# Closing of a hybrid decoder layer: sample outputs stored feature by token, feature tiles transposed two down tiles behind

## The chip, the core and the metric

The kernel runs on one core of a Trainium2 chip. Five engines work side by side and meet through semaphores: PE (TensorE, products and transposes into PSUM), DVE (VectorE), ACT (ScalarE), POOL (GpSimd) and SP (SyncE, which here only issues DMA transfers). The metric is device time in microseconds, the median of several executions. A trace of one execution gives each instruction's start and duration; its first instruction to its last is the span.

## The reference

One layer of a decoder serves 512 prompt tokens and 32 sample tokens (8 sequences of 4) with shared weights. The part that matters here is the end of the layer, the second feed-forward network with its norms:

```
def rmsnorm(x, g):
    y = xf * lax.rsqrt(jnp.mean(xf * xf, axis=-1, keepdims=True) + EPS)
    return (y * g.astype(jnp.float32)).astype(x.dtype)

def swiglu(x, wg, wu, wd):
    return (jax.nn.silu(x @ wg) * (x @ wu)) @ wd

    h = h + rmsnorm(m, norm_g[3])
    h = h + 0.5 * rmsnorm(swiglu(rmsnorm(h, norm_g[4]), wg[1], wu[1], wd[1]), norm_g[5])
```

The model width is 1024 and the inner width 2816, all in 32-bit floats. The results are the tokens' new rows (512 x 1024 for the prompt, 32 x 1024 for the samples) and caches and states that are stored much earlier in the program.

## The kernel before

**Layout.** Activations lie feature by token: 1024 features are 8 tiles of 128 partitions, and tokens run along the free dimension. The 544 tokens are cut in two halves. Half a has 256 prompt tokens and is finished and stored first, still feature by token (`y_a`). Half b has 256 prompt tokens and the 32 sample tokens behind them, 288 columns, and is the last work of the program. Its prompt outputs `y_p` and its sample outputs `y_s` are stored token by feature, so its feature tiles have to be transposed on PE.

**Products.** Each product of two 32-bit matrices is made of three passes over parts: weights are split on chip into a high part `wh` (a cast on ACT, L248) and a low part `wl` (a subtraction on DVE, L249), activations in the same way (`uhb`, `ulb` and, inside the network, `hhb`, `hlb` by L168 and L169). `mm3` (L257) then issues high by high, low by high and high by low for each of the 128-deep slices: 24 products for a gate or up tile (8 slices), 15 for a tile of the last down chunk (5 slices).

**The second feed-forward network of half b** (`ffn` with `fin`): the inner width is cut in four chunks of 6, 6, 5 and 5 tiles. In each chunk, gate and up tiles are computed and joined (L348, L318 to L320, L350, L351), and then 8 down tiles, one for each feature tile d, are added into `mT` (`mb` in the profile, L376). In the last chunk each tile is finished at once: ACT squares it (L296) and scales it by the norm's weights (L299), and DVE sums the squares into `ssmb` (L298).

**The closing** (class `Finish`, called from `ffn`). What sets the order of work on an engine is the order in which the program issues it, as the tile scheduler lays it out; every engine runs its own list in order.

- `begin` turns the row of first-norm factors `rnb` (one per token, the same in all partitions) into columns with one number per token and partition: `turn` makes products with one column, two for the 128-token groups (L1512) and four copies for the 32 sample tokens (L1514).
- `hold` transposes the residual `hb` ahead of time: sixteen 128 x 128 transposes (L1537) and, by `small` (L1527), eight products of 32 by 128 for the sample tokens, which ACT copies out of PSUM (L1538, L1542). Both stand at the seam, among the first gate and up tiles of this network.
- `column` transposes one finished feature tile: two transposes (L1550) and a `small` (L1527). It runs `LAG` tiles behind the down tile, with `LAG` = 3. At feature tile 3 ACT copies the first four columns out (`mt`, L1552), so that their PSUM banks come free.
- `sums` and `scale` add the squares over all features (`turn` again, once for the sum of the first seven tiles and once for the last square `sq`) and compute the scale of the norm, `sT` (L1562 to L1565).
- `end` multiplies and adds the residual, in four pieces of 128 tokens by 512 features (L1577, one of them by ACT and POOL, L1574 and L1575), stores each (L1578), and does the same for the samples (L1580), which leave in four stores of 32 rows (L1582).

SP's queue issues all weight loads and most stores; two of the sample stores and one prompt store go by ACT's queue. The columns that are left when the last tile is done come behind the last sums:

```
if last and fin and LAG <= d < KD - 1:
    fin.column(mT[x], d - LAG)
if last and grp is groups[-1] and fin:
    with tc.issue_after(fin.scale(sq).ins):
        for d in range(KD - LAG - 1, KD):
            fin.column(mT[x], d)
    fin.end()
```

So columns 0 to 3 stand in the loop over down tiles (behind tiles 3 to 6), and columns 4 to 7 behind the last sums.

Of the kernel before, what the change touches and what calls it, by code (L numbers as in the profile page):

```python
# [8 lines left out]
F32 = mybir.dt.float32  # L9
# [39 lines left out]
DP = 6  # L49
LAG, BEG = 3, 0  # L50
PJ0, LOOK = 4, 1
# [57 lines left out]
def hybrid_step_kernel(  # L109
# [212 lines left out]
    def ffn(i, n_post, xs, u, nxt=None, mid=None, late=None, fin=None, pre=(), fine=False):  # L322
# [5 lines left out]
        for c, (f0, nf) in enumerate(FCH[i]):  # L328
# [31 lines left out]
            for grp in groups:  # L360
# [7 lines left out]
                for x in xs:  # L368
                    for d in grp:
                        acc = accs[0] if accs else gemm(wts[d], (hh[x], hl[x]))  # L370
                        if last and fin and d == KD - 1:
                            fin.sums(sacc[x])
                        if c == 0:
                            nc.scalar.copy(mT[x][:, d], acc)
                        else:
                            nc.vector.tensor_tensor(mT[x][:, d], mT[x][:, d], acc, op=ALU.add)  # L376
# [1132 lines left out]
    class Finish:  # L1509
        def turn(self, pr, t, one, start=True, stop=True):  # L1510
            for i in range(2):
                nc.tensor.matmul(pr[:, i : i + 1], t[:, i * P : (i + 1) * P], one, start=start and i == 0, stop=stop, skip_group_check=True)  # L1512
            for g in range(0, P, TS):
                ins = nc.tensor.matmul(pr[g : g + TS, 2:3], t[:, 2 * P :], one, start=False, stop=stop, skip_group_check=True)  # L1514
            return ins

        def begin(self, r):
            self.rT = mk([P, 3], F32, "rT")
            self.r2T = mk([P, 3], F32, "r2T")
            pr = ps("pr", PRT)  # L1520
            self.turn(pr, r, ident[:, :1])
            nc.vector.tensor_copy(self.rT, pr[:, :3])
            nc.vector.tensor_tensor(self.r2T, self.rT, self.rT, op=ALU.mult)

        def small(self, out, m, d):
            g = d // 2 * TS
            nc.tensor.matmul(out[g : g + TS, d % 2 * P : (d % 2 + 1) * P], m[:, d, 2 * P :], ident, start=True, stop=True, skip_group_check=True)  # L1527

        def hold(self):
            ht = mk([P, 2 * KQ * HS[1]], F32, "q1", pool=dK)  # L1530
            self.ht = [ht[:, i * D : (i + 1) * D] for i in range(2)] + [ht[:, 2 * D : 2 * D + 256]]
            self.mt = [mk([P, 512], F32, "mt", 2) for _ in range(2)]
            for i in range(2):
                for q in range(2):
# [3 lines left out]
                    nc.scalar.copy(self.ht[i][:, q * 512 : (q + 1) * 512], py)  # L1538
            py = ps("py")
            for d in range(KD):  # L1540
                self.small(py, h[1], d)
            nc.scalar.copy(self.ht[2], py[:, :256])  # L1542

        def column(self, m, d):
            if d % 4 == 0:
                self.py = [ps("py") for _ in range(2)]
            if d == 0:
                self.ps_ = ps("py")
            for i in range(2):
                nc.tensor.transpose(self.py[i][:, d % 4 * P : (d % 4 + 1) * P], m[:, d, i * P : (i + 1) * P], ident)  # L1550
                if d == 3:
                    nc.scalar.copy(self.mt[i], self.py[i])  # L1552
            self.small(self.ps_, m, d)

        def sums(self, acc):
            self.pr = ps("pr", PRT)
            self.turn(self.pr, acc, ones[:, :1], stop=False)

        def scale(self, sq):
            pin = self.turn(self.pr, sq, ones[:, :1], start=False)  # L1560
            t = self.t = mk([P, 3], F32, "sT")
            nc.vector.scalar_tensor_tensor(t, self.pr[:, :3], 1.0 / D, self.r2T, op0=ALU.mult, op1=ALU.mult)  # L1562
            nc.scalar.activation(t, t, AF.Ln, scale=1.0, bias=epst)
# [3 lines left out]

        def end(self):
            t = self.t
            for i, q in ((0, 0), (1, 0), (0, 1), (1, 1)):  # L1570
                qs = slice(q * 512, (q + 1) * 512)
                y = self.ht[i][:, qs]
                if (i, q) == (1, 0):
                    nc.scalar.mul(self.mt[1], self.mt[1], t[:, 1:2])  # L1574
# [3 lines left out]
                (nc.scalar if i > q else nc.sync).dma_start(y_p[i * P : (i + 1) * P, qs], y)  # L1578
            y = self.ht[2]
            nc.vector.scalar_tensor_tensor(y, self.ps_[:, :256], t[:, 2:3], y, op0=ALU.mult, op1=ALU.add)  # L1580
            for g in range(4):
                (nc.scalar, nc.sync)[g % 2].dma_start(y_s[:, g * 256 : (g + 1) * 256], y[g * TS : (g + 1) * TS])  # L1582

# [44 lines left out]
_OUTS = [  # L1628
    (P, KD, HS[0]), (TP - HS[0], D), (TS, D),
    (P, 2, TP), (RD, TP), (NH, P, P),  # L1630
# [9 lines left out]
def _outputs(y_a, y_p, y_s, ckv_p, kr_p, st_p, ckv_s, kr_s, st_s):  # L1640
    y_p = np.concatenate([y_a.transpose(2, 1, 0).reshape(HS[0], D), y_p])
    return (
        y_p.reshape(1, TP, D), y_s.reshape(NB, NT, D),
        np.ascontiguousarray(ckv_p.transpose(2, 1, 0)).reshape(1, 1, TP, R), np.ascontiguousarray(kr_p.T).reshape(1, 1, TP, RD),
# [46 lines left out]
```

## Time and profile before

| | us |
|---|---|
| median of 3 executions (lowest, highest) | 1271.8 (1271.74, 1272.26) |
| the profiled execution, whole | 1272.22 |
| its span | 1270.4 |
| PE busy in the span | 1250.7 |
| DVE, ACT, POOL busy | 982.6, 741.2, 75.9 |
| mean granted clock of PE, share of full | 0.994 |

Busy time says how much of the span an engine had an instruction in it. The chain of waits is followed back from the last instruction, at each step to what released it; its parts add up to the span. In a timeline a row is a start, a duration, engine, line, operation, `out<-in` by the program's names and shapes, and in brackets how long the engine stood idle before it and what ended that. PE's instructions overlap in their pipeline, so the time from one start to the next is what one costs in a stream, not its duration. A 32-bit transpose is one record; a 32-bit product that is no split part is two passes and has two records, each with its own load of weights.

### The profile page before, as it was taken

To read this page: it belongs to the slowest core of one execution; us is meant where nothing else is said; L and a number is where in the kernel's file an instruction comes from. 1 tells how busy PE (TensorE), PEld (TensorE's weight loads), DVE (VectorE), ACT (ScalarE), POOL (GpSimd) and SP (SyncE) were. 2 spreads that over 40 slices of the span, in tenths; PEclk is the share of its full clock that TensorE was granted. 3 is DMA by queue.
4 is the path that set the end of the run, shared out by engine and by line. 5 is a ranking of instruction groups with operands and counts; after the bars stand their busy time and mean duration, and the time that the engine had idled before them with its cause. 6 is when DMAs were issued, how large, how long until landed. Compare 5 with 4: busy or idle time off the path is not lost.

```text
span 1270.4 us, 30188 instructions
## 1 busy us (share of the span) xinstructions
PE 1250.7 (98%) x12442; PEld 1159.4 (91%) x12442; DVE 982.6 (77%) x1972; ACT 741.2 (58%) x1560; POOL 75.9 (6%) x80
## 2 busy tenths in 40 slices
PE   8999999999999999999999999999999999999998
PEld 7999999999999988889888888788788999999996
DVE  7897778888678887767766898989987778566664
ACT  7665545454566644546557655664656776554454
POOL 0000000000000000000000422322300000000000
PEclk9999999999999999999999899999999999999998
DMA  6233323332254221223223978878676635545541
GB/s 233 84 117 100 100 84 100 101 100 92 54 218 157 78 90 59 80 78 127 80 85 102 345 254 298 286 263 316 240 267 209 193 113 178 189 133 187 157 144 49
DMA packets 73018, 195.08 MB, mean 154 GB/s; under 512 B 12368, under 2 KB 27760, under 8 KB 68144
## 3 DMA queue, kind: packets, MB, share of 16 engines
q1 hardware_dynamic: 64320, 149.88, 36.3%
q0 software_dynamic: 7168, 41.95, 9.0%
q8 instruction: 98, 1.61, 0.5%
q10 hardware_dynamic: 1392, 1.32, 0.4%
q14 instruction: 40, 0.33, 0.1%
HBM read 183.45 MB, written 9.67 MB: 152 GB/s over the span
## 4 chain that ended last, share of the span: by engine, by line
PE 88%; DVE 6%; ACT 5%; issue 1%; DMA 0%; SPq 0%; DVEq 0%; ACTq 0%
PE acc L257 29%; PE acc L275 18%; PE dn L257 8%; PE Y L559 6%; PE X L559 4%; PE Z L559 4%; PE s L1375 3%; PE acc L715 3%; PE o L1408 2%; DVE wl L249 1%; PE s L1188 1%; PE pa L931 1%; PE acc L286 1%; ACT wh L248 1%; DVE kh L1363 1%
## 5 line engine op out<-in xcount | busy, mean ns | idle before, releaser
L248 ACT CAST wh<-wraw 128x1024 fp32r<-128x1024 f32 (+2 forms) x194 | 185.1, 957 | 185.5 <-PE acc L257 117.9
L249 DVE TENSOR_TENSOR wl<-wraw,wh 128x1024 fp32r<-128x1024 f32 (+2 forms) x194 | 214.5, 1107 | 82.6 <-ACT wh L248 82.2
L275 PE MATMUL acc<-uha,wh 128*128 128x256 f32 (+1 forms) x528 | 159.3, 302 | 0.9 <-ACT uha L205 0.9
L275 PE MATMUL acc<-ula,wh 128*128 128x256 f32 (+1 forms) x528 | 151.5, 287 | 0.0
L275 PE MATMUL acc<-uha,wl 128*128 128x256 f32 (+1 forms) x528 | 150.3, 285 | 0.8 <-DVE wl L249 0.7
L257 PE MATMUL acc<-uhb,wh 128*128 128x288 f32 (+1 forms) x432 | 128.2, 297 | 0.0
L257 PE MATMUL acc<-ulb,wh 128*128 128x288 f32 (+1 forms) x432 | 127.5, 295 | 0.0
L257 PE MATMUL acc<-uhb,wl 128*128 128x288 f32 (+1 forms) x432 | 126.8, 295 | 0.6 <-DVE wl L249 0.3
L275 PEld LDWEIGHTS acc<-uha,wh 128*128 128x128 f32 x528 | 100.1, 190 | 15.2 <-issue 13.2
L275 PEld LDWEIGHTS acc<-uha,wl 128*128 128x128 f32 x528 | 100.1, 190 | 1.6 <-DVE wl L249 1.3
L275 PEld LDWEIGHTS acc<-ula,wh 128*128 128x128 f32 x528 | 100.5, 190 | 1.0 <-issue 1.0
L257 PEld LDWEIGHTS acc<-uhb,wl 128*128 128x128 f32 x432 | 81.2, 188 | 1.3 <-DVE wl L249 1.3
L257 PEld LDWEIGHTS acc<-uhb,wh 128*128 128x128 f32 x432 | 81.0, 187 | 0.7 <-ACT wh L248 0.3
L257 PEld LDWEIGHTS acc<-ulb,wh 128*128 128x128 f32 x432 | 81.1, 188 | 0.1
L257 PE MATMUL dn<-hh,dh 128*128 128x272 f32 x256 | 74.3, 290 | 0.0
L257 PE MATMUL dn<-hh,dl 128*128 128x272 f32 x256 | 73.7, 288 | 0.0
L257 PE MATMUL dn<-hl,dh 128*128 128x272 f32 x256 | 73.6, 288 | 0.0
L1399 ACT COPY pbuf<-pt 32x64 f32<-32x64 f32 x192 | 46.5, 242 | 13.3 <-DVE pt L1395 10.6
L1375 PE MATMUL s<-kh,q 64*32 64x128 f32 x2560 | 54.0, 275 | 0.0
L275 PE MATMUL acc<-uhb,wh 128*128 128x272 f32 x176 | 53.3, 303 | 0.0
L257 PE MATMUL acc<-hlb,wh 128*128 128x288 f32 x176 | 52.1, 297 | 0.0
L257 PE MATMUL acc<-hhb,wh 128*128 128x288 f32 x176 | 51.8, 298 | 0.0
(642 smaller groups left out, 3904.7 us busy)
## 6 DMA issues: line engine op xcount, KB each, us to landing
wraw<-w_u SPq DMA_DIRECT2D x66, 512.0 KB, 3.5
wraw<-w_g SPq DMA_DIRECT2D x65, 512.0 KB, 4.0
wraw<-w_d SPq DMA_DIRECT2D x40, 384.0 KB, 3.3
wraw<-w_in SPq DMA_DIRECT2D x24, 512.0 KB, 3.6
wraw<-w_d SPq DMA_DIRECT2D x32, 320.0 KB, 2.9
wraw<-w_d SPq DMA_DIRECT2D x16, 512.0 KB, 4.0
wraw<-w_o SPq DMA_DIRECT2D x16, 512.0 KB, 4.0
g_S<-state SPq DMA_DIRECT2D x4, 512.0 KB, 4.0
```

Of the source, the lines that this page charges most:

```text
L248: nc.scalar.copy(wh[:, :kt], w[:, :kt])
L249: nc.vector.tensor_tensor(wl[:, :kt], w[:, :kt], f32(wh[:, :kt]), op=ALU.subtract)
L257: nc.tensor.matmul(out, a, b, start=n == 0, stop=n == last)
L275: nc.tensor.matmul(acc[:, :n], a[:, k], b[:, k], start=k + i == 0, stop=k == kt - 1 and i == 2)
L286: nc.tensor.matmul(acc, a[:, k], b[:, k], start=k + i == 0, stop=k == kt - 1 and i == 2)
L559: nc.tensor.matmul(bank, a[p][:, k], b[q][:, k], start=first and k + n == 0, stop=k == 3 and n == 2, skip_group_check=True)
L715: nc.tensor.matmul(accs[x, d], wts[d][p][:, k], hs[k // 2][q][:, k % 2, x], start=k + n == 0, stop=k == nf - 1 and n == 2)
L931: nc.tensor.matmul(pa[es, c * 32 : (c + 1) * 32].rearrange("p (n m) -> p n m", m=m), kx[:, cs], up(qx[:, cs]), start=True, stop=True, skip ...
L1188: nc.tensor.matmul(s[:, :N], qa[a_], ka[b_], start=n == 0, stop=False, skip_group_check=True)
L1375: nc.tensor.matmul(self.s[r][c * 32 : c * 32 + 32, :P], q[rs, j], kh, start=st + jj == 0, stop=st == len(JS) - 1 and jj == 1, skip_group_c ...
L1399: (nc.scalar.copy if g else nc.vector.tensor_copy)(self.p[g * 32 : g * 32 + 32, c // 2, c % 2 * 4 : c % 2 * 4 + 4, self.i * 16 : self.i * ...
L1408: nc.tensor.matmul(o[g : g + 32, :R], self.p[:, c, a], self.craw[c][:, a], start=i + c == 0 and a < 4, stop=i + c == 2 and a >= 4, skip_gr ...
```

## The change

`LAG` becomes 2, so column d - 2 follows down tile d, and column 5 now follows tile 7, between the first sums and the last; two columns are left behind the last sums. The sample tokens are no longer transposed at all. Their part of `mT` and of the residual stays feature by token, the norm's factors for them are kept as 32 numbers in every partition (columns 2 to 33 of `rT`, `r2T` and `sT`), and the sums for them come from a product with a full matrix of ones (L1548 of the new file). Their result is made by two operations of DVE on 128 partitions by 8 x 32 and stored by one transfer of 128 KB, feature by token; the host turns it around when it unpacks the outputs, as it does for `y_a`.

```
-LAG, BEG = 3, 0
+LAG, BEG = 2, 0
...
-                        if last and fin and LAG <= d < KD - 1:
+                        if last and fin and LAG <= d:
                             fin.column(mT[x], d - LAG)
                     if last and grp is groups[-1] and fin:
                         with tc.issue_after(fin.scale(sq).ins):
-                            for d in range(KD - LAG - 1, KD):
+                            for d in range(KD - LAG, KD):
                                 fin.column(mT[x], d)
-                        fin.end()
+                        fin.end(mT[x])
...
         def turn(self, pr, t, one, start=True, stop=True):
             for i in range(2):
                 nc.tensor.matmul(pr[:, i : i + 1], t[:, i * P : (i + 1) * P], one, start=start and i == 0, stop=stop, skip_group_check=True)
-            for g in range(0, P, TS):
-                ins = nc.tensor.matmul(pr[g : g + TS, 2:3], t[:, 2 * P :], one, start=False, stop=stop, skip_group_check=True)
-            return ins
...
-            nc.vector.tensor_copy(self.rT, pr[:, :3])
+            nc.vector.tensor_copy(self.rT[:, :2], pr[:, :2])
+            nc.vector.tensor_copy(self.rT[:, 2:], r[:, 2 * P :])
...
-        def small(self, out, m, d):
-            g = d // 2 * TS
-            nc.tensor.matmul(out[g : g + TS, d % 2 * P : (d % 2 + 1) * P], m[:, d, 2 * P :], ident, start=True, stop=True, skip_group_check=True)
...
-            py = ps("py")
-            for d in range(KD):
-                self.small(py, h[1], d)
-            nc.scalar.copy(self.ht[2], py[:, :256])
...
-            self.small(self.ps_, m, d)
...
+        def both(self, t, last=False):
+            self.turn(self.pr, t, ones[:, :1], start=not last, stop=last)
+            return nc.tensor.matmul(self.pr[:, 2 : 2 + TS], ones, t[:, 2 * P :], start=False, stop=last, skip_group_check=True)
...
-        def end(self):
+        def end(self, m):
             t = self.t
+            ys = mk([P, KD, TS], F32, "ys")
             for i, q in ((0, 0), (1, 0), (0, 1), (1, 1)):
                 qs = slice(q * 512, (q + 1) * 512)
                 y = self.ht[i][:, qs]
+                if (i, q) == (0, 1):
+                    nc.vector.tensor_tensor(ys, m[:, :, 2 * P :], t[:, None, 2:].broadcast_to([P, KD, TS]), op=ALU.mult)
+                    nc.vector.tensor_tensor(ys, ys, h[1][:, :, 2 * P :], op=ALU.add)
+                    nc.sync.dma_start(y_s, ys)
...
-            y = self.ht[2]
-            nc.vector.scalar_tensor_tensor(y, self.ps_[:, :256], t[:, 2:3], y, op0=ALU.mult, op1=ALU.add)
-            for g in range(4):
-                (nc.scalar, nc.sync)[g % 2].dma_start(y_s[:, g * 256 : (g + 1) * 256], y[g * TS : (g + 1) * TS])
```

**The seam.** PE's list there, before the change. `py` are PSUM tiles of transposes, `pr` the turned factors, `acc` the accumulator of one gate or up tile; the tile of `acc_14391` has 24 products, of which the first three and the last two are shown, and `acc_14422` is the next tile, B.

```order
L1537 MATMUL py_14360<-ident_67,hb_13389 128x128 x4
L1527 MATMUL py_14366<-ident_67,hb_13389 32x128 x8
L257 MATMUL acc_14391<-uhb_14005,wh_14386 128x288
L257 MATMUL acc_14391<-ulb_14006,wh_14386 128x288
L257 MATMUL acc_14391<-uhb_14005,wl_14387 128x288
...
L257 MATMUL acc_14391<-ulb_14006,wh_14386 128x288
L257 MATMUL acc_14391<-uhb_14005,wl_14387 128x288
L1512 MATMUL pr_14675<-ident_67,rnb_14007 128x1 x2
L1514 MATMUL pr_14675<-ident_67,rnb_14007 32x1 x4
L257 MATMUL acc_14422<-uhb_14005,wh_14417 128x288
L257 MATMUL acc_14422<-ulb_14006,wh_14417 128x288
```

PE's list at the same place after the change; lines and buffer numbers are those of the new file, `acc_14381` is the first tile and `acc_14412` is B.

```order
L1531 MATMUL py_14360<-ident_67,hb_13389 128x128 x4
L257 MATMUL acc_14381<-uhb_14005,wh_14376 128x288
L257 MATMUL acc_14381<-ulb_14006,wh_14376 128x288
L1512 MATMUL pr_14665<-ident_67,rnb_14007 128x1 x2
L257 MATMUL acc_14381<-uhb_14005,wl_14377 128x288
...
L257 MATMUL acc_14381<-ulb_14006,wh_14376 128x288
L257 MATMUL acc_14381<-uhb_14005,wl_14377 128x288
L257 MATMUL acc_14412<-uhb_14005,wh_14407 128x288
L257 MATMUL acc_14412<-ulb_14006,wh_14407 128x288
L257 MATMUL acc_14412<-uhb_14005,wl_14408 128x288
```

The eight sample products and the four of the turn are gone, and the turn stands ahead of the first product that needs a low part. DVE's list there, before (`wl_14418` is B's low part):

```order
L311 TENSOR_TENSOR ha_13384<-ha_13384,ma_8872 128x512
L169 TENSOR_TENSOR hlb_14166<-sil_14257,hhb_14165 128x288
L169 TENSOR_TENSOR hlb_14166<-sil_14329,hhb_14165 128x288
L348 TENSOR_TENSOR sil_14447<-acc_14391,rnb_14007 128x288
L249 TENSOR_TENSOR wl_14418<-wraw_14416,wh_14417 128x1024
L249 TENSOR_TENSOR wl_14459<-wraw_14457,wh_14458 128x1024
```

And after (`wl_14408` is B's low part):

```order
L311 TENSOR_TENSOR ha_13384<-ha_13384,ma_8872 128x512
L1519 COPY rT_14663<-pr_14665 128x2
L249 TENSOR_TENSOR wl_14408<-wraw_14406,wh_14407 128x1024
L169 TENSOR_TENSOR hlb_14166<-sil_14257,hhb_14165 128x288
L169 TENSOR_TENSOR hlb_14166<-sil_14329,hhb_14165 128x288
L348 TENSOR_TENSOR sil_14437<-acc_14381,rnb_14007 128x288
L249 TENSOR_TENSOR wl_14449<-wraw_14447,wh_14448 128x1024
```

B's low part moved ahead of the two `hlb` and of L348, behind a copy of the turned factors. On ACT the cast of B's high part moved in the same way, to the place right behind the copies of `hold`.

**The closing.** PE's list from the end of the last down tile, before (`ssmb` is the sum of the first squares, `sq1` the last square; the rows of columns 5 and 6, which read like those of column 4, are left out):

```order
L1512 MATMUL pr_16669<-ones_70,ssmb_16442 128x1 x2
L1514 MATMUL pr_16669<-ones_70,ssmb_16442 32x1 x4
L1512 MATMUL pr_16669<-ones_70,sq1_16677 128x1 x2
L1514 MATMUL pr_16669<-ones_70,sq1_16677 32x1 x4
L1550 MATMUL py_16691<-ident_67,mb_14164 128x128
L1550 MATMUL py_16692<-ident_67,mb_14164 128x128
L1527 MATMUL py_16551<-ident_67,mb_14164 32x128
...
L1550 MATMUL py_16691<-ident_67,mb_14164 128x128
L1550 MATMUL py_16692<-ident_67,mb_14164 128x128
L1527 MATMUL py_16551<-ident_67,mb_14164 32x128
```

After:

```order
L1512 MATMUL pr_16655<-ones_70,ssmb_16429 128x1 x2
L1548 MATMUL pr_16655<-ssmb_16429,ones_70 128x32
L1538 MATMUL py_16629<-ident_67,mb_14164 128x128
L1538 MATMUL py_16630<-ident_67,mb_14164 128x128
L1512 MATMUL pr_16655<-ones_70,sq1_16660 128x1 x2
L1548 MATMUL pr_16655<-sq1_16660,ones_70 128x32
L1538 MATMUL py_16629<-ident_67,mb_14164 128x128
L1538 MATMUL py_16630<-ident_67,mb_14164 128x128
L1538 MATMUL py_16629<-ident_67,mb_14164 128x128
L1538 MATMUL py_16630<-ident_67,mb_14164 128x128
```

Column 5 stands between the two sums, and columns 6 and 7 behind them. DVE's end of the program after the change:

```order
L1553 SCALAR_TENSOR_TENSOR sT_16668<-pr_16655,r2T_14664 128x34
L1556 TENSOR_TENSOR sT_16668<-sT_16668,rT_14663 128x34
L1573 SCALAR_TENSOR_TENSOR q1_14339<-mt_14340,sT_16668,q1_14339 128x512
L1566 TENSOR_TENSOR ys_16677<-mb_14164,sT_16668 128x256
L1573 SCALAR_TENSOR_TENSOR q1_14339<-py_16629,sT_16668,q1_14339 128x512
L1567 TENSOR_TENSOR ys_16677<-ys_16677,hb_13389 128x256
L1573 SCALAR_TENSOR_TENSOR q1_14339<-py_16630,sT_16668,q1_14339 128x512
```

Before, the three of 128x512 followed each other and one of 128x256 came last (L1580). The two sample operations now lie between the wide ones. On SP the sample store follows the second wide piece's and comes ahead of the last one's.

More of the change, by code (lines that the diff above doesn't have):

```diff
@@ L1512, in turn @@
                 nc.tensor.matmul(pr[:, i : i + 1], t[:, i * P : (i + 1) * P], one, start=start and i == 0, stop=stop, skip_group_check=True)
-            for g in range(0, P, TS):
-                ins = nc.tensor.matmul(pr[g : g + TS, 2:3], t[:, 2 * P :], one, start=False, stop=stop, skip_group_check=True)
-            return ins
         def begin(self, r):
-            self.rT = mk([P, 3], F32, "rT")
-            self.r2T = mk([P, 3], F32, "r2T")
+            self.rT = mk([P, 2 + TS], F32, "rT")
+            self.r2T = mk([P, 2 + TS], F32, "r2T")
             pr = ps("pr", PRT)
             self.turn(pr, r, ident[:, :1])
-            nc.vector.tensor_copy(self.rT, pr[:, :3])
+            nc.vector.tensor_copy(self.rT[:, :2], pr[:, :2])
+            nc.vector.tensor_copy(self.rT[:, 2:], r[:, 2 * P :])
             nc.vector.tensor_tensor(self.r2T, self.rT, self.rT, op=ALU.mult)
-        def small(self, out, m, d):
-            g = d // 2 * TS
-            nc.tensor.matmul(out[g : g + TS, d % 2 * P : (d % 2 + 1) * P], m[:, d, 2 * P :], ident, start=True, stop=True, skip_group_check=True)
         def hold(self):
             ht = mk([P, 2 * KQ * HS[1]], F32, "q1", pool=dK)
-            self.ht = [ht[:, i * D : (i + 1) * D] for i in range(2)] + [ht[:, 2 * D : 2 * D + 256]]
+            self.ht = [ht[:, i * D : (i + 1) * D] for i in range(2)]
             self.mt = [mk([P, 512], F32, "mt", 2) for _ in range(2)]
@@ L1552, in column @@
                     nc.scalar.copy(self.mt[i], self.py[i])
-            self.small(self.ps_, m, d)
         def sums(self, acc):
             self.pr = ps("pr", PRT)
-            self.turn(self.pr, acc, ones[:, :1], stop=False)
+            self.both(acc)
+        def both(self, t, last=False):
+            self.turn(self.pr, t, ones[:, :1], start=not last, stop=last)
+            return nc.tensor.matmul(self.pr[:, 2 : 2 + TS], ones, t[:, 2 * P :], start=False, stop=last, skip_group_check=True)
         def scale(self, sq):
-            pin = self.turn(self.pr, sq, ones[:, :1], start=False)
-            t = self.t = mk([P, 3], F32, "sT")
-            nc.vector.scalar_tensor_tensor(t, self.pr[:, :3], 1.0 / D, self.r2T, op0=ALU.mult, op1=ALU.mult)
+            pin = self.both(sq, True)
+            t = self.t = mk([P, 2 + TS], F32, "sT")
+            nc.vector.scalar_tensor_tensor(t, self.pr[:, : 2 + TS], 1.0 / D, self.r2T, op0=ALU.mult, op1=ALU.mult)
             nc.scalar.activation(t, t, AF.Ln, scale=1.0, bias=epst)
@@ L1628 @@
 _OUTS = [
-    (P, KD, HS[0]), (TP - HS[0], D), (TS, D),
+    (P, KD, HS[0]), (TP - HS[0], D), (P, KD, TS),
     (P, 2, TP), (RD, TP), (NH, P, P),
@@ L1642, in _outputs @@
     return (
-        y_p.reshape(1, TP, D), y_s.reshape(NB, NT, D),
+        y_p.reshape(1, TP, D), np.ascontiguousarray(y_s.transpose(2, 1, 0)).reshape(NB, NT, D),
         np.ascontiguousarray(ckv_p.transpose(2, 1, 0)).reshape(1, 1, TP, R), np.ascontiguousarray(kr_p.T).reshape(1, 1, TP, RD),
```

2 lines of the change are left out of this document (removed).

## The prediction

> **What bounds the kernel now.** I read the page first (shares and the chain of work that ended last), then the chain over the last 35 us, then the timelines of the engines at the two places that the change touches: the seam before the second feed-forward network (1053 to 1061 us) and the closing (from 1244 us).
>
> ```profile
> span 1270.4 us, 30188 instructions
> PE 1250.7 (98%) x12442; PEld 1159.4 (91%) x12442; DVE 982.6 (77%) x1972; ACT 741.2 (58%) x1560; POOL 75.9 (6%) x80
> PE 88%; DVE 6%; ACT 5%; issue 1%; DMA 0%; SPq 0%; DVEq 0%; ACTq 0%
> ```
>
> PE carries 88% of the chain, so an instruction that leaves PE's queue shortens the span unless PE waits there for something else. The chain of waits near the end (start, us, what):
>
> ```profile
> 1251.22 0.22 PE py L1550 x2
> 1251.44 0.34 PE py L1527 x2
> 1251.78 2.19 PE acc L257 x15
> 1253.96 0.22 PE py L1550 x2
> ...
> 1259.48 0.47 DVE mb L376
> 1259.97 0.45 ACT sq L296
> 1260.46 0.61 PE pr L1512 x4
> 1261.07 0.17 PE pr L1514 x8
> ...
> 1264.80 1.41 DVE q L1577 x2
> ```
>
> Up to 1259.4 PE alone sets the pace: a column of transposes (L1550), the same column of the sample tokens (L1527), fifteen products of a down tile. Then one pass goes through DVE, ACT and PE for the last norm; four columns that were left over keep PE busy, and DVE can only start the last two 512-wide results at 1264.80.
>
> **The change part by part. First, the loop over down tiles.** The adds of DVE show the step of a tile that carries no column:
>
> ```profile
> 1244.52 0.45 DVE L376 TENSOR_TENSOR mb<-mb,acc 128x288 f32<-128x288 f32 x1 [0.28 <-PE acc L257]
> 1246.52 0.45 DVE L376 TENSOR_TENSOR mb<-mb,acc 128x288 f32<-128x288 f32 x1 [0.18 <-PE acc L257]
> ```
>
> That is 2.00 us, 0.133 per product. With a column the step is 1253.96 - 1251.22 = 2.74, so a column costs 0.74, four of them 2.96. What of it is the sample product that goes away? PE's timeline:
>
> ```profile
> 1248.63 0.41 PE L1527 MATMUL py<-ident,mb 128*32 128x128 f32 x2
> 1248.96 0.40 PE L257 MATMUL acc<-hhb,wh 128*128 128x288 f32 x1
> ```
>
> From its start to the next product are 0.33. Without it a column costs 0.41, if the way from a transpose to a product is as long as that from a transpose to the small product. With two tiles behind instead of three, five columns stand in the loop: 5 x 0.41 = 2.05, a gain of **0.91**. The trace has no transpose that runs straight into a product without another wait, so both ends: if the switch is free, only the 0.22 of the transposes is left, 1.10 for five, a gain of 1.86; if it costs again the 0.19 by which 2.19 exceeds 2.00, five columns cost 3.0 and the gain is nil. I take 0.91, the nearer row. The column two tiles behind needs ACT's scaling (L299) of a tile that PE finished over 4 us earlier, so it adds no wait.
>
> **Second, the seam.** Here the residual is transposed (L1537), eight sample products follow (L1527), and the reciprocals are turned (L1512, L1514).
>
> ```profile
> 1053.17 1.47 PE L1537 MATMUL py<-ident,hb 128*128 128x128 f32 x12
> 1054.57 0.66 PE L1527 MATMUL py<-ident,hb 128*32 128x128 f32 x16
> 1055.16 0.41 PE L257 MATMUL acc<-uhb,wh 128*128 128x288 f32 x1
> 1056.00 0.40 PE L257 MATMUL acc<-uhb,wl 128*128 128x288 f32 x1 [0.30 <-DVE wl L249]
> 1059.05 0.50 PE L1512 MATMUL pr<-ident,rnb 128*128 128x1 f32 x4
> 1060.89 0.40 PE L257 MATMUL acc<-uhb,wl 128*128 128x288 f32 x1
> ```
>
> Deleting the 0.59 of L1527 gives nothing by itself: PE only reaches the wait that ends at 1056.00 earlier, since DVE is the late one. But the turn now stands in that hole (0.6 long, after two products), so the tile that runs 1056.00 to 1059.05 is followed at once by the next, B. What B needs comes from here:
>
> ```profile
> 1055.80 1.53 ACT L1538 COPY q<-py 128x512 f32<-128x512 f32 x3
> 1057.22 0.38 ACT L1542 COPY q<-py 128x256 f32<-128x256 f32 x1
> 1058.15 2.00 ACT L248 CAST wh<-wraw 128x1024 fp32r<-128x1024 f32 x2
> 1057.33 0.68 DVE L311 TENSOR_TENSOR ha<-ha,ma 128x512 f32<-128x512 f32 x1
> 1059.62 4.62 DVE L249 TENSOR_TENSOR wl<-wraw,wh 128x1024 fp32r<-128x1024 f32 x4
> ```
>
> L1542 goes, and B's cast comes right after the copies: 1057.2 plus about 1.05 is 1058.27. DVE ends L311 at 1058.01, copies the turned reciprocals, starts B's split (now ahead of two hlb) at 1058.3 and ends it 1.23 later, at 1059.53. PE starts B's low product at about 1059.57 with two products ahead of it, instead of 1060.89 with four: 1.32 - 2 x 0.133 = **1.05** gained. The split after it follows two hlb and one more operation and should end near 1061.8; PE wants it near 1062.9. The DVE copy that now waits for the turn holds B's split behind it, but the turn ends near 1055.7, two us ahead of that copy. Ends: nil, if PE waits out the same time for the splits behind B; 1.3, if B's split also came in time.
>
> **Third, the closing.** Rows:
>
> ```profile
> 1262.27 0.75 DVE L1577 SCALAR_TENSOR_TENSOR q<-mt,sT,q 128x512 f32<-128x512 f32 x1
> 1263.12 1.26 POOL L1575 TENSOR_TENSOR q<-q,mt 128x512 f32<-128x512 f32 x1 [329.30 <-ACT mt L1574]
> L298 DVE TENSOR_TENSOR ssma<-ssma,sq 128x256 f32<-128x256 f32 x7 | 2.9, 417 | 0.1
> L1582 SPq DMA_DIRECT2D out<-q x2: 395/410/426, 1266.7 to 1267.1; - x2
> DMA to landing us min/median/max: 2.0/2.1/2.1
> 1264.00:1264.50 0.50, 0.50 (x3) 0.22 (x2) 0.00 (x0) 0.00 (x0) 0.38 (x1) 0.50 0.98 381
> ```
>
> Now the last sample store is issued at 1267.1 and lands at 1269.1; 1.3 us later the span ends. After the change: one column and the sums fill the 0.5 in which PE waited for ACT's square (L296), so they cost nothing as long as they end by 1260.46 (about 0.43 + 0.27 + 0.4 from 1259.28). The last sums replace eight passes (0.17) by two against a full set of weights, 0.04 to 0.27 (from the eight short ones, and from L1512's four in 0.54). Four small operations grow from 3 to 34 columns, about 0.03 each. So DVE's first result starts some 0.2 later, at 1262.47. Two columns are left on PE; four with their sample products took 3.6 (1261.24 to 1264.80), so two end by 1263.2, before DVE asks at 1263.46. It runs 512, 256, 512, 256, 512 wide: starts are 0.66 apart after a wide one (1.41 - 0.75) and 0.33 after a 256 (417 ns less the same overlap). The second wide result ends at 1264.21, the last at 1265.21. Stores, 0.04 later: alone the last would land at 1265.25 + 2.1 = 1267.35. But the transfers share a rate: 381 GB/s is 0.69 us for 262 KB. The store issued at 1264.25 lands at 1266.35, and 131 + 262 + 262 KB behind it take 1.72 more: 1268.07. Against 1269.1 that is **1.05** gained; ends 1.75 (the rate does not bind) and 0.5 (every 0.1 of delay before DVE's first result costs 0.1, and I allow 0.5 for what is not shown).
>
> Three stores fewer are issued, and a 128 KB one is added on SP ahead of the last; its 0.4 of issue ends before the last result is ready.
>
> DVE is idle now while POOL adds (1263.12); afterwards two of DVE's operations with both inputs in SBUF run beside it. [...] No row here shows the two together. [...]
>
> **Sum.** 0.91 + 1.05 + 1.05 = 3.0. The profiled execution took 1272.22 (span 1270.4 and 1.8 around it), which is 0.4 above the median of 1271.8; 3.0 off its 1272.2 is 1269.2, and off the median 1268.8.
>
> **The rivals.** (a) The seam is hidden: ACT and DVE stay the late ones behind B too. For it: both are busy nearly all of 1056 to 1061. Against it: the margin of about 1 us above. Then 1.96 is left: 1269.8.
>
> (b) The switch from transpose to product is free: 0.95 more, 1267.8.
>
> (c) The store of the sample tile goes out in short pieces, as the tile is eight runs of 32 numbers.
>
> ```profile
> wraw<-w_g SPq DMA_DIRECT2D x2, 256.0 KB, 3.0
> wraw<-w_kr SPq DMA_DIRECT2D x2, 256.0 KB, 4.9
> ```
>
> The same bytes in quarter-width pieces took 1.9 longer. The last store, behind it on SP, would land at 1269.97: closing +0.87 instead of -1.05, in all 1270.7. Against it: both sides of the store are contiguous in each partition.
>
> (d) Slower: the clock falls at the seam. Rows of granted clock (last three numbers: clock, DMA share, GB/s):
>
> ```profile
> 1053.00:1056.00 3.00, 2.70 (x33) 2.09 (x32) 3.00 (x6) 3.00 (x8) 0.00 (x0) 1.00 0.00 0
> 1261.70:1261.90 0.20, 0.20 (x2) 0.00 (x0) 0.00 (x0) 0.17 (x2) 0.00 (x0) 0.70 0.00 0
> 1268.50:1270.40 1.90, 0.00 (x0) 0.00 (x0) 0.00 (x0) 0.00 (x0) 0.00 (x0) 0.50 0.00 0
> ```
>
> In the closing the clock halved at about 1261.8, 2.4 us after the last dense product, and stayed so to the end, 8.6 us. At the seam 2.8 us lie between dense products (1053.17 to 1056.00, bar two), and the change takes the 0.59 of small products out of them. Half clock for 8.6 us would lose 4.3 there: 1273.1. It decides the sign from 6 us on. Against it: the same stretch, just as long, kept 1.00. [...]
>
> **How the numbers follow.** Forecast with all three terms 0.60; (a) 0.17; (b) 0.10; (c) 0.07; (d) 0.06. The predicted time is the forecast's, 1268.8. Bounds of the terms together reach from 1266.9 to 1271.3; not all fall one way, so the range is 1267.4 to 1270.8, which takes in (a), (b) and (c) and leaves out (d). About 0.2% is what a measurement of this kernel can tell from no change; 0.2% faster is 1269.3. Faster: nearly all of the forecast and all of (b), 0.67. Within: the slow edge of the forecast, (a), (c), half of (d), 0.30. Slower: 0.03.
>
> **What would show it.** Right: the step of a down tile with a column falls from 2.74 to about 2.41; PE's gap at 1059 to 1061 shrinks to some 0.3; DVE does not wait before its second wide result; the last store lands about 1.1 sooner after the last product. Wrong: a step of 2.6 or 2.2; PE waiting for L249 again behind B; a long first wait at the last pr; sample stores in thousands of packets; a clock below 1.00 between 1054 and 1062.

## The result and the profile after

| | before | after |
|---|---|---|
| median of 6 executions each, us | 1272.03 (1271.6 to 1272.77) | 1266.86 (1266.67 to 1267.99) |
| the profiled execution, its span | 1272.22, 1270.4 | 1266.67, 1264.9 |

The ratio on record for the changed kernel's time is 0.9965 (95% interval 0.9956 to 0.9975); the quotient of the two medians in the table is 0.9959. By the medians it takes 5.2 us less, between the two profiled executions 5.5 less. The forecast was 3.0 less, 1268.8, with a range of 1267.4 to 1270.8; the median lies 0.5 below that range. The page of the changed kernel, its span, its busy times and the shares of the chain of waits:

```profile
span 1264.9 us, 30079 instructions
...
PE 1242.6 (98%) x12390; PEld 1155.9 (91%) x12390; DVE 982.9 (78%) x1974; ACT 741.0 (59%) x1559; POOL 75.5 (6%) x80
...
PE 87%; DVE 6%; ACT 5%; issue 1%; DMA 0%; DVEq 0%; SPq 0%; ACTq 0%
```

PE was busy 1250.7 before and 1242.6 now, with 52 records fewer: it still bounds the kernel. The chain of waits near the end, after the change (start, us, what):

```profile
1246.39 0.22 PE py L1538 x2
1246.61 2.00 PE acc L257 x15
1248.61 0.22 PE py L1538 x2
...
1255.31 0.47 DVE mb L376
...
1258.26 0.75 DVE q L1573
1259.01 0.34 DVE ys L1566
1259.34 0.66 DVE q L1573
1260.01 0.74 DVEq L1679
1260.75 0.66 DVE q L1573
```

A step of a down tile with a column is now 1248.61 - 1246.39 = 2.22. Before it was 2.74, and a tile without a column takes 2.00: so a column costs 0.22, nothing but its two transposes. The closing is DVE's from 1258.26 on, without the wait for PE that stood at 1264.80 before. The seam, from the timelines of PE, ACT and DVE after the change:

```profile
1051.90 1.47 PE L1531 MATMUL py<-ident,hb 128*128 128x128 f32 x12
1053.48 0.50 PE L1512 MATMUL pr<-ident,rnb 128*128 128x1 f32 x4
1054.72 0.40 PE L257 MATMUL acc<-uhb,wl 128*128 128x288 f32 x1 [0.74 <-DVE wl L249]
1058.31 0.40 PE L257 MATMUL acc<-uhb,wl 128*128 128x288 f32 x1
...
1055.93 1.06 ACT L248 CAST wh<-wraw 128x1024 fp32r<-128x1024 f32 x1
...
1057.02 1.23 DVE L249 TENSOR_TENSOR wl<-wraw,wh 128x1024 fp32r<-128x1024 f32 x1 [0.22 <-ACT wh L248]
```

The low product of the next tile, B, starts at 1058.31, that is 6.41 behind the residual's first transposes. Before it was 1060.89 - 1053.17 = 7.72.

**Where the 5.5 went.** Three landmarks cut an execution: the residual's first transposes, DVE's last addition of a down tile (`mb`, L376), and the end of the span.

| us | before | after | gain |
|---|---|---|---|
| first transposes | 1053.17 | 1051.90 | 1.27 |
| from there to the last addition (1259.48; 1255.31) | 206.31 | 203.41 | 2.90 |
| from there to the end (1270.4; 1264.9) | 10.92 | 9.59 | 1.33 |

Of the 2.90, the loop has 1.86 (four columns of 0.74 against five of 0.22); the other 1.04 are the seam's, where B's low product gained 7.72 - 6.41 = 1.31 with two products of 0.133 fewer ahead of it. Spans are given to 0.1 us, so a closing or a stretch to the end may be off by 0.05, and a difference of two by 0.1.

The first row is no part of the change: up to there both programs are the same. Up to 700 us the two executions run level (one split of L249 on DVE starts at 699.01 before and at 699.12 after), and at 740 us the changed one is ahead (a later split starts at 741.37 before and at 740.14 after). Between the two, about 708 us, the views by stretches of 2 us show the granted clock (last three numbers: clock, DMA share, GB/s). Before, and then after:

```profile
708.00:710.00 2.00, 1.06 (x6) 0.77 (x5) 2.00 (x5) 1.32 (x4) 1.69 (x2) 0.70 0.98 393
710.00:712.00 2.00, 2.00 (x11) 2.00 (x11) 2.00 (x6) 1.31 (x4) 1.15 (x2) 0.50 1.02 422
712.00:714.00 2.00, 2.00 (x11) 2.00 (x11) 2.00 (x5) 1.45 (x3) 0.00 (x0) 0.50 0.96 406
714.00:716.00 2.00, 2.00 (x12) 2.00 (x12) 1.86 (x6) 1.77 (x5) 0.00 (x0) 0.59 1.00 350
```

```profile
708.00:710.00 2.00, 1.03 (x5) 0.59 (x5) 2.00 (x5) 1.21 (x3) 1.70 (x2) 0.90 0.98 410
710.00:712.00 2.00, 1.99 (x10) 1.99 (x10) 2.00 (x5) 1.42 (x5) 1.26 (x2) 0.50 1.03 430
712.00:714.00 2.00, 2.00 (x15) 2.00 (x15) 2.00 (x5) 1.34 (x3) 0.00 (x0) 0.75 1.01 426
```

PE is busy 1.06 and 1.03 of the 2.00 us from 708, and the clock falls to 0.50. What it lacks of full speed over these rows is 2.00 x (0.30 + 0.50 + 0.50 + 0.41) = 3.42 us before and 2.00 x (0.10 + 0.50 + 0.25) = 1.70 after: the half clock lasted 6.8 us in the one execution and 3.4 in the other. The stretch from the first transposes to the end is therefore the better measure of the change: 217.2 before, 213.0 after, 4.2 gained.

### The profile page after: what moved, and what is told of

Same layout as the page of the kernel before. It is cut to its first block, busy times and chain, and to the rows that moved or that the text cites. A ratio compares the mean times of both kernels' runs of the same rounds, so it can differ in the third digit from the quotient of the medians.

```text
span 1264.9 us, 30079 instructions
## 1 busy us (share of the span) xinstructions
PE 1242.6 (98%) x12390; PEld 1155.9 (91%) x12390; DVE 982.9 (78%) x1974; ACT 741.0 (59%) x1559; POOL 75.5 (6%) x80
## 2 busy tenths in 40 slices
DMA packets 72969, 195.06 MB, mean 154 GB/s; under 512 B 12320, under 2 KB 27712, under 8 KB 68096
## 4 chain that ended last, share of the span: by engine, by line
PE 87%; DVE 6%; ACT 5%; issue 1%; DMA 0%; DVEq 0%; SPq 0%; ACTq 0%
PE acc L257 30%; PE acc L275 17%; PE dn L257 8%; PE Y L559 6%; PE X L559 4%; PE Z L559 4%; PE acc L715 3%; PE s L1375 3%; PE o L1408 2%; DVE wl L249 1%; DVE kh L1363 1%; PE s L1188 1%; PE pa L931 1%; ACT wh L248 1%; PE acc L286 1%
## 5 line engine op out<-in xcount | busy, mean ns | idle before, releaser
L249 DVE TENSOR_TENSOR wl<-wraw,wh 128x1024 fp32r<-128x1024 f32 (+2 forms) x194 | 214.5, 1107 | 82.8 <-ACT wh L248 82.4
L1399 ACT COPY pbuf<-pt 32x64 f32<-32x64 f32 x192 | 46.5, 242 | 13.3 <-DVE pt L1395 10.6
```

Of the source, the lines that this page charges most:

```text
L249: nc.vector.tensor_tensor(wl[:, :kt], w[:, :kt], f32(wh[:, :kt]), op=ALU.subtract)
L1399: (nc.scalar.copy if g else nc.vector.tensor_copy)(self.p[g * 32 : g * 32 + 32, c // 2, c % 2 * 4 : c % 2 * 4 + 4, self.i * 16 : self.i * ...
```

## The experiments

All stretches below are counted from the residual's first transposes ("stretch") or from DVE's last addition ("closing"). Each kernel of an experiment was profiled once; those of experiment 10 were also timed over more executions. Experiments 1, 2, 3 and 5 were made on one chip, 4 on a second, 6 to 9 on a third and 10 on a fourth. The stretches of the two unchanged kernels, profiled again in experiment 10, came out within 0.4 (before) and 0.1 (changed) of the first ones.

**1. The sample product ahead of the transposes.** In the kernel before:

```
         def column(self, m, d):
...
+            self.small(self.ps_, m, d)
             for i in range(2):
                 nc.tensor.transpose(...)
...
-            self.small(self.ps_, m, d)
```

> The kernel before with one order turned round: in each column the sample product stands ahead of the two transposes instead of behind them. Nothing is left out. A (a switch is paid where a two-pass product is followed by a product of split operands; the way from a transpose to such a product is free): a column falls from 0.74 us to about 0.30 (0.22 for two transposes and 0.07 for the two passes), the step of a down tile with a column from 2.74 to about 2.30, and the stretch from the first transposes of the residual to the end of the span from 217.2 to about 215. B (a sample product costs its 0.52 wherever it stands): the step stays at 2.74 and the stretch at 217.2. In between (a switch of its own from the sample product to the transposes): 2.4 to 2.6.

Its chain of waits:

```profile
1253.42 0.34 PE py L1527 x2
1253.75 0.37 PE py L1551 x2
1254.12 1.99 PE acc L257 x15
1256.11 0.34 PE py L1527 x2
```

The step is 1256.11 - 1253.42 = 2.69, the stretch 1269.5 - 1052.72 = 216.8. B holds, and A fell: 0.05 of a column went, not 0.44. The rows show how the cost is made up. The sample product takes 0.34 in either place. What follows it starts 0.15 to 0.19 late: the transposes here (0.37 instead of 0.22), the split products before (2.19 instead of 2.00). The split products behind transposes take 1.99, so that way is free.

**2. The sample products of the residual deleted in the kernel before**, with ACT's copy of them:

```
-            py = ps("py")
-            for d in range(KD):
-                self.small(py, h[1], d)
-            nc.scalar.copy(self.ht[2], py[:, :256])
```

> The kernel before without the eight sample products of the residual ahead of the second network, and without the copy behind them; the last sample result is then only scaled, so the sample outputs lack their residual. Loop and closing keep their forms. A (the turn that comes ahead of the hole, and B's low weights ahead of two hlb, are the gain at the seam; the products' own 0.59 is hidden): product with A's low weights no nearer to the transposes than 2.83 us, B's low product about 1.05 sooner behind the transposes than in the kernel before (7.72 there), stretch 216.2. B (the deleted 0.59 counts by itself): stretch 216.6, with B's wait as long as before. C (both): 215.6.

PE's timeline there (first transposes at 1052.77):

```profile
1054.35 0.50 PE L1512 MATMUL pr<-ident,rnb 128*128 128x1 f32 x4
1055.60 0.41 PE L257 MATMUL acc<-uhb,wl 128*128 128x288 f32 x1 [0.57 <-DVE wl L249]
1059.18 0.40 PE L257 MATMUL acc<-uhb,wl 128*128 128x288 f32 x1
```

The low product of the tile ahead of B stays 2.83 behind the transposes, and B's comes at 6.41 instead of 7.72. To DVE's last addition (1258.05) it is 205.28 against 206.31: 1.03 gained by this deletion alone, as in A. With the closing of this execution the stretch is 216.3.

**3. The same products put back into the changed kernel, without the copy:**

```
+            py = ps("py")
+            for d in range(KD):
+                g = d // 2 * TS
+                nc.tensor.matmul(py[g : g + TS, ...], h[1][:, d, 2 * P :], ident, ...)
```

> The changed kernel with the eight sample products of the residual put back behind its transposes, written to a buffer that nobody reads; the turn then stands about 27 products later on PE. A (the 0.59 lies in the wait for A's low weights): the product with A's low weights stays 2.82 us behind the first transposes, B's low product at about 6.4 (it was 6.41), plus at most 0.2 for the turn in the stream; stretch 213.0 to 213.3. B (the 0.59 counts by itself): 3.4 and 7.0, stretch 213.6. C (the early turn is what brings B's weights in time): B's low product at about 7.4, stretch 214.0.

PE's timeline:

```profile
1052.16 1.47 PE L1531 MATMUL py<-ident,hb 128*128 128x128 f32 x12
1053.56 0.66 PE L1536 MATMUL py<-ident,hb 128*32 128x128 f32 x16
1054.99 0.41 PE L257 MATMUL acc<-uhb,wl 128*128 128x288 f32 x1 [0.30 <-DVE wl L249]
1058.29 0.50 PE L1512 MATMUL pr<-ident,rnb 128*128 128x1 f32 x4
1058.65 0.38 PE L257 MATMUL acc<-uhb,wl 128*128 128x288 f32 x1
```

The low product ahead of B comes at 2.83, B's at 6.49, and the stretch is 1265.2 - 1052.16 = 213.0. So PE's 0.59 are worth nothing, and neither is the early place of the turn: here L1512 stands behind the whole tile again.

**4. The products and ACT's copy put back** (the edit of experiment 3 and one line):

```
+            nc.scalar.copy(ht[:, 2 * D : 2 * D + 256], py[:, :256])
```

> The changed kernel with the eight sample products of the residual put back, and with ScalarE's copy of them too, into a place that nobody reads. A (what the seam gained is the place in ScalarE's queue that this copy held, ahead of the cast of B's weights, and with it the place of B's split ahead of two hlb on DVE): the cast comes behind the copy and the two hhb again, the split behind L348, B's low product at about 7.7 us behind the residual's first transposes as in the kernel before, stretch 214.0 to 214.3 against 213.0. B (only PE's 0.59 or the place of the turn counted, which the run with the products alone showed to be nothing): 6.4 to 6.5, stretch 213.0 to 213.1.

PE, ACT and DVE (first transposes at 1052.31):

```profile
1060.01 0.40 PE L257 MATMUL acc<-uhb,wl 128*128 128x288 f32 x1
...
1056.35 0.38 ACT L1537 COPY q<-py 128x256 f32<-128x256 f32 x1
1056.61 0.78 ACT L168 CAST hhb<-sil 128x288 fp32r<-128x288 f32 x2
1057.28 2.00 ACT L248 CAST wh<-wraw 128x1024 fp32r<-128x1024 f32 x2
...
1058.37 0.46 DVE L348 TENSOR_TENSOR sil<-acc,rnb 128x288 f32<-128x288 f32 x1 [0.35 <-PE acc L257]
1058.74 4.62 DVE L249 TENSOR_TENSOR wl<-wraw,wh 128x1024 fp32r<-128x1024 f32 x4
```

B's low product is back at 7.70, and the stretch is 214.0. The whole gain of the seam hangs on one copy of 0.38 us on ACT. With it the scheduler puts two `hhb` ahead of the cast of B's weights, which starts 4.97 behind the transposes instead of 4.03, and DVE's split behind L348, which waits for PE: it starts at 6.43 instead of 5.12. Of the 0.94 by which the cast is later, these starts give 0.26 to the copy and 0.67 to the two `hhb` (1056.35, 1056.61, 1057.28). No run has the copy without the changed order, so what the copy alone would cost is not shown.

**5. The lag alone**, in the kernel before with its sample products:

```
-LAG, BEG = 3, 0
+LAG, BEG = 2, 0
...
-                        if last and fin and LAG <= d < KD - 1:
+                        if last and fin and LAG <= d:
...
-                            for d in range(KD - LAG - 1, KD):
+                            for d in range(KD - LAG, KD):
```

> The kernel before with the columns two tiles behind instead of three, sample products kept: one more column in the loop, one between the two sums, two behind the last sum. A (the columns left over at half clock hold DVE's last two results, 1262.27 + 0.75 to 1264.80): loop +0.74, DVE without that wait, stores then bound by their rate (918 KB behind the first at 381 GB/s), closing about 1.5 shorter; stretch 216.5 against 217.2. B (the stores bind whatever DVE does): stretch 218.0. C (the column between the sums delays the last norm by its 0.7): 217.2.

To the last addition it is 207.02 against 206.31, the forecast extra column; the closing is 9.99 against 10.92; the stretch 217.0. DVE has no wait left (its two wide results run from 1263.19 on), and then the transfers bind. One of the stretches of half a microsecond in which they run without a break:

```profile
1266.00:1266.50 0.50, 0.00 (x0) 0.00 (x0) 0.00 (x0) 0.00 (x0) 0.00 (x0) 1.00 1.04 389
```

A has the mechanism, but not its size: 0.9 of the 1.5 came. Not all of that is the lag's, for the clock kept full speed until 7 us behind the last addition here and halved after 2.3 in the kernel before. In experiment 1, with the columns three tiles behind and the clock full for 9 us, the closing is 1269.5 - 1258.85 = 10.65; against that the shorter lag gains 0.7. C's delay is 0.12 (the first wide result starts 2.91 behind the last addition instead of 2.79). Net, the lag by itself gains no more than the 0.4 by which two executions of the kernel before differ (217.2, and 216.8 in experiment 10).

**6. Without POOL's addition**, in the changed kernel:

```
-                    nc.gpsimd.tensor_tensor(y, y, self.mt[1], op=ALU.add)
+                    y = self.mt[1]
```

> The changed kernel without POOL's addition in the closing: the second half of the token rows is stored without its residual in the first 512 features, and its store no longer waits for POOL. A (the second sample operation waits for POOL because both read SBUF): that operation takes about 0.42 us instead of 0.83, DVE's last wide result starts 0.4 sooner. B (its operand, every eighth block of the residual, is what makes it slow): it stays at 0.83. The stretch from the last DVE addition of a down tile to the end of the span was 9.59; with the store from ScalarE's queue no longer behind POOL the hole in the transfers (143 GB/s in half a microsecond) fills and it should be 9.2 to 9.3.

On the chip of this run and the next three the kernel before took 1282.68; the four profiled executions are 10 to 11 us longer there between about 720 and 975 us, far ahead of both landmarks. DVE and POOL in the changed kernel, and then DVE in this one:

```profile
1258.93 0.42 DVE L1566 TENSOR_TENSOR ys<-mb,sT 128x256 f32<-128x256 f32 x1
1259.12 1.35 POOL L1571 TENSOR_TENSOR q<-q,mt 128x512 f32<-128x512 f32 x1 [326.53 <-ACT mt L1570]
...
1259.92 0.83 DVE L1567 TENSOR_TENSOR ys<-ys,hb 128x256 f32<-128x256 f32 x1
```

```profile
1270.70 0.42 DVE L1567 TENSOR_TENSOR ys<-ys,hb 128x256 f32<-128x256 f32 x1
```

With POOL busy until 1260.47, the addition takes 0.83; without POOL, 0.42 on the same operands. A's 0.42 came and B fell; that SBUF is where the two meet, as A has it, is not shown. The closing is 1275.3 - 1266.08 = 9.22.

**7 and 8. The sample operations behind the wide ones.** Experiment 7 moves only the second operation and the store, experiment 8 (its second diff, in addition to the first) both operations:

```
-                    nc.vector.tensor_tensor(ys, ys, h[1][:, :, 2 * P :], op=ALU.add)
-                    nc.sync.dma_start(y_s, ys)
...
+            nc.vector.tensor_tensor(ys, ys, h[1][:, :, 2 * P :], op=ALU.add)
+            nc.sync.dma_start(y_s, ys)
```

```
-                    nc.vector.tensor_tensor(ys, m[:, :, 2 * P :], ..., op=ALU.mult)
...
+            nc.vector.tensor_tensor(ys, m[:, :, 2 * P :], ..., op=ALU.mult)
```

> The changed kernel with the second sample operation and the sample store put behind the last wide result. A (the transfers bind from the second store on): the operation takes about 0.42, DVE's last wide result ends 0.75 sooner, and the end moves by less than 0.1: closing 9.5 to 9.6 against 9.59. B (DVE's last result binds): closing about 9.2 or, by the wide result alone, 8.9.

> The changed kernel with both sample operations and the sample store put behind the last wide result. A (the transfers bind, and their only hole is the wait for the second store): the second store is issued 0.33 sooner, the hole goes, closing 9.2 to 9.3 against 9.59, all else the same. B (DVE's last result binds): it ends at the same time as in the changed kernel less the 0.41 of the wait for POOL, and only a 128 KB store follows, closing about 9.0.

In experiment 7 the last wide result ends 0.73 sooner behind the last addition (5.37 instead of 6.10), and the closing is 1276.4 - 1266.84 = 9.56, which is no change that a span given to 0.1 can show. In experiment 8 it is 1275.1 - 1265.82 = 9.28, 0.31 less. A holds in both. The transfers of the changed kernel and then of experiment 8, in stretches of half a microsecond:

```profile
1260.00:1260.50 0.50, 0.00 (x0) 0.00 (x0) 0.50 (x2) 0.00 (x0) 0.46 (x1) 0.50 0.99 385
1260.50:1261.00 0.50, 0.00 (x0) 0.00 (x0) 0.50 (x2) 0.00 (x0) 0.00 (x0) 0.50 0.38 143
1261.00:1261.50 0.50, 0.00 (x0) 0.00 (x0) 0.41 (x1) 0.00 (x0) 0.00 (x0) 0.50 1.03 381
```

```profile
1271.00:1271.50 0.50, 0.00 (x0) 0.00 (x0) 0.47 (x2) 0.00 (x0) 0.00 (x0) 0.88 1.00 377
1271.50:1272.00 0.50, 0.00 (x0) 0.00 (x0) 0.14 (x1) 0.00 (x0) 0.00 (x0) 0.50 1.01 377
```

The changed kernel has a hole of about 0.3 us (143 of 385 GB/s) while the second store is still to come. Experiment 7 has the same hole (143 GB/s from 1272.0 to 1272.5) and keeps its closing; experiments 6 and 8, which fill it, shorten the closing by 0.3 to 0.4.

**9. Three tiles behind again**, in the changed kernel (`LAG, BEG = 3, 0`):

> The changed kernel with the columns three tiles behind again: four in the loop, one between the sums, three behind the last sum. A (a column without sample product costs 0.22 in the loop and nothing in the closing, where PE ended 1.6 before DVE asked): step 2.22, one step fewer with a column, stretch from the residual's first transposes 212.8 against 213.0, closing 9.59. B (the columns left over hold DVE again, as in the kernel before): closing 9.7 or more.

To the last addition it is 203.19 against 203.41, the closing 9.54 against 9.59 (the same within 0.1), the stretch 212.7. A holds: with cheap columns the shorter lag costs a column in the loop, 0.22, and gives nothing back.

**10. Both of these together** (experiments 8 and 9), over more executions, beside the two kernels as they are:

> The changed kernel with both that gained something by the trace: columns three tiles behind, and both sample operations with their store behind the last wide result. If the two add up: stretch from the residual's first transposes 212.5 (213.0 - 0.22 - 0.31), so 0.5 below the changed kernel in time. If the left-over columns now hold DVE (three columns end about 0.2 before DVE asks 0.33 sooner): 212.7 or more.

> The changed kernel once more, as it is. Stretch from the residual's first transposes 213.0. A (of the 5.5 between the two profiles 1.28 came from the halved clock near 708 us, which falls once or twice in an execution whatever the kernel): medians over many executions differ by 4.2 to 4.7, ratio 0.9963 to 0.9967 against the kernel before. B (the change itself makes the earlier part shorter): 5.2 to 5.5, ratio 0.9957 to 0.9959.

> The kernel before once more, as it is, against itself. Stretch 217.2. A (the number of halved stretches near 708 us is chance): ratio within 0.0007 of 1, and the profile may show one stretch of 3.4 us or two. B (it belongs to the kernel before): two stretches, 6.8 us, as in its first profile.

| | executions | median (lowest, highest) | stretch | ratio to before (95%) |
|---|---|---|---|---|
| before | 18 | 1271.88 (1270.12, 1274.81) | | |
| before, once more | 12 | 1271.69 (1270.52, 1274.23) | 216.8 | 0.9996 (0.9987 to 1.0006) |
| changed | 7 | 1267.97 (1266.44, 1268.92) | 212.9 | 0.9965 (0.9951 to 0.9978) |
| changed, both edits | 6 | 1266.91 (1265.60, 1267.57) | 212.5 | 0.9957 (0.9942 to 0.9971) |

The two edits add up in the stretch (212.5 as forecast). In time the combination lies 1.1 below the changed kernel by the medians, but the two intervals overlap: that it is faster is shown by the trace, not by the times. The changed kernel is 3.9 below the one before here, a little less than case A, and the ratio, 0.9965, is A's. Its interval holds B's ratios too; what speaks against B is the second pair of profiles, in which the residual's first transposes come at 1054.18 in the changed kernel and at 1052.09 in the one before, later and not sooner. The expectation B for the kernel before is wrong, and so is "once or twice in an execution", by the views of the clock in its second profile and in the changed kernel's:

```profile
710.00:712.00 2.00, 1.84 (x15) 1.64 (x15) 2.00 (x6) 1.88 (x6) 1.70 (x2) 1.00 1.01 426
```

```profile
710.00:712.00 2.00, 2.00 (x11) 2.00 (x11) 2.00 (x6) 1.15 (x4) 1.03 (x1) 0.50 1.03 430
```

This time the kernel before kept its full clock there, and the changed one had the half clock for 6.8 us. Between these two profiled executions (1270.63 and 1268.92) lie only 1.7 us, though their stretches differ by 3.9.

## Why the prediction was right, and where it was wrong

**The loop, forecast 0.91, measured 1.86.** This is the step that failed: "a column costs 0.41, if the way from a transpose to a product is as long as that from a transpose to the small product". It is not. The way from a transpose to a split product is free (the fifteen products behind transposes took 2.00, as in a tile without a column), and a column costs 0.22. The condition was named as unproved, and the free switch, rival (b), was given a tenth; it is what happened. Experiment 1 shows what stood in its place: the 0.52 between 0.74 and 0.22 belong to the sample product wherever it stands, 0.34 for it and 0.15 to 0.19 for whatever comes next. My first theory behind that, a switch that only the split products pay, fell in the same run.

**The seam, forecast 1.05, measured 1.04.** The times inside it came as forecast, counted 1.27 earlier for the start: B's cast at 1055.93 (1057.2 forecast), its split at 1057.02 (1058.3), its low product at 1058.31 (1059.57). That the 0.59 of the products give nothing by itself is shown by experiment 3. Half of the reason was wrong, though: the turn's move into the hole, named first, is worth at most 0.08 (6.49 against 6.41 with the turn late). What counts is the other half, "L1542 goes, and B's cast comes right after the copies" (experiment 4). PE's gap ahead of B's low product shrank to some 0.3, as forecast, and rival (a) fell.

**The closing, forecast 1.05, measured 1.33 between the profiles.** Point by point: DVE's first result starts 2.95 behind the last addition instead of 2.79, 0.16 later (0.2 forecast). DVE does not wait before its second wide result. The rate of the transfers sets the last landing (377 to 389 GB/s from 1270.5 to 1273.0 in experiment 8): experiments 7 and 8 show it, and the trace of experiment 5 agrees. The 1.05 was worked out for this landing. It comes 8.53 behind the last addition (1261.44 + 2.4 = 1263.84) where it came 9.6 behind it (1269.1), so it is right for this pair of profiles. The other 0.3 was not in the sum, which let the span end 1.3 behind the last landing as before; now it ends about 1.0 behind it. At the end of the program SP's queue waits for semaphores one after another, and fewer of these waits stand behind the last landing. Before, and after:

```profile
L1687 SPq EVENT_SEMAPHORE  x10: 17/28/28, 1269.1 to 1270.4; - x10
```

```profile
L1679 SPq EVENT_SEMAPHORE  x5: 17/28/28, 1263.9 to 1264.8; - x5
```

In the trace they start 0.06 apart just behind the landing, and five fewer make 0.3. No run varied them alone.

The size is softer than it looks: a second profile of the kernel before has a closing of 1268.9 - 1258.35 = 10.55: its clock halved 0.9 later behind the last addition, and the left-over columns held DVE for 1.22 instead of 1.78. Against 9.54 to 9.59 that is 1.0 gained, of which the waits at the end are again 0.3 and the landing only some 0.6 to 0.7. So the phase of the clock leaves 0.4 of the landing's gain open, and how well 1.05 fits the first pair is in part luck.

**POOL beside DVE**, of which the prediction had no row: DVE's second sample operation took 0.83 beside POOL's addition and 0.42 without it (experiment 6). The 0.41 hardly moves the end: in experiment 7 the operation comes behind POOL's addition and takes 0.42, and the closing is 9.56 against 9.59.

**The other rivals.** The transfers of the changed kernel and a row of its clock at the seam:

```profile
out<-ys SPq DMA_DIRECT2D x1, 128.0 KB, 2.4
```

```profile
1054.00:1056.00 2.00, 1.28 (x9) 1.28 (x10) 2.00 (x5) 2.00 (x6) 0.00 (x0) 1.00 0.16 33
```

The sample store landed 2.4 us after its issue, 0.3 more than the 2.1 of the last stores before, not 1.9 more, and the whole program has 49 packets fewer (73018 and 72969), not thousands more: (c) fell. The clock stayed at 1.00 there, and to 1062: (d) fell.

**What the sum left out.** Three terms sum to 3.0; the trace has 1.86 + 1.04 + 1.0 to 1.3, which is 3.9 to 4.2, and the medians over more executions differ by 3.9. The loop lacks 0.95 of that, and the waits at the end of the program 0.3. The further 1.27 of the first pair of profiles comes from the stretch about 708 us. That the first medians differ by 5.2 for the same reason is likely and not shown, as the other executions were not profiled: in experiment 10 the four executions of the kernel before with a mean clock of 0.993 took 1274.5 to 1274.8, and those with 0.997 or more 1270.1 to 1272.0. The prediction had no term for such differences; a single profile may differ by 2 us in code that nobody touched (the residual's first transposes came at 1051.90 and at 1054.18 in the two profiles of the changed kernel).

**The lag**, in the prediction part of the loop's and the closing's sums, is worth nothing in itself. With the old columns the 0.7 to 0.9 that it gains in the closing is paid with 0.7 in the loop (experiment 5); with the new ones it costs 0.22 (experiment 9). The gain of this change is the sample tokens', which no longer pass through PE.

## What to carry to other kernels

A short two-pass product that stood alone among split products cost several times its passes here (0.34 us to the next start and 0.15 to 0.19 more for what follows; 0.07 to the next start where eight stood together), so gather such products or do without them; transposes in the same stream cost only their own 0.11 each. Where weights are cast and split just in time, look at every small operation queued ahead of the cast, however far from the engine that waits: 0.38 us on ACT decided 1.0 on PE. Compare two kernels by the stretch behind the first instruction that differs, not by the spans of two profiles.

## What the runs showed that was not expected

- **Half clock at one place, of chance length.** Over the 14 profiles the half clock near 708 us lasts 0, 3.4 or 6.8 us (what it lacks is 0, 1.70 or 3.42): none in 2, one length in 9, two in 3, for both kernels. Against two lengths, none brought the following instructions 2.0 us forward in the second profile of the kernel before, and one 1.0 to 1.3. By 740 us the distance between two executions has changed by up to another 0.9, of which the cause is open.
- **The closing's clock has a phase too.** It halved 2.3 us behind the last addition in the first profile of the kernel before, 3.2 in the second, and only after 7 in experiment 5. The left-over columns take PE 3.6 us (1261.24 to 1264.80) in the first, and 2.6 (1260.61 to 1263.23) at full clock in experiment 1.
- **Another chip, 11 us longer.** In experiments 6 to 9 the profiled executions were 10 to 11 us longer between 720 and 975, with the clock at 1.00 and hardly a wait of the products themselves (1.0 us in all in experiment 8). Most of it stands ahead of the weight loads of one line, the products of L1408 in a part of the layer far from this change: there PE's load queue was idle 12.2 to 13.3 us in these four profiles and 4.6 in the changed kernel's first, each time with nothing in the profile that ended the wait. Why is open.
